# RWKV-7 and chunk-band attention trunk on one core: two pairs of heads side by side, and the key projections in one stretch

## The chip, the cores and the metric

One core of a Trainium2 chip runs the whole program. The metric is the device time of one execution in microseconds; of the kernel before there are three runs, 2769.82, 2777.21 and 2778.8 us, and one profiled execution.

## The reference

The input x is 256 tokens of 2048 elements in fp32. There are two layers. Layer 0 mixes over time (RWKV-7, 32 heads of 64) and has an MLP; then keys and values are projected once from the stream; layer 1 attends to those in a band of chunks and has another MLP. Each sub-layer stands behind an RMSNorm with shift and scale, and in front of a gate, all three from products c @ w_ada. The part that the change touches is this:

```python
    r = xr @ w_r
    k = xk @ w_k
    v = xv @ w_v
    w_log = -jax.nn.softplus(-(w0 + jnp.tanh(xw @ w1) @ w2)) - 0.5
    a = jax.nn.sigmoid(a0 + (xa @ a1) @ a2)
    g = jax.nn.sigmoid(xg @ g1) @ g2
    kk = heads(k * k_k)
    kk = kk / jnp.maximum(jnp.sqrt(jnp.sum(kk * kk, axis=-1, keepdims=True)), 1e-12)
    k = k * (1 + (a - 1) * k_a)
    decay = jnp.exp(-jnp.exp(heads(w_log)))
    ...
        sa = jnp.einsum('bhvk,bhk->bhv', S, -kk_t)
        S = (S * w_t[:, :, None, :] + sa[..., None] * (kk_t * a_t)[:, :, None, :]
             + v_t[..., None] * k_t[:, :, None, :])
        y = jnp.einsum('bhvk,bhk->bhv', S, r_t)
    ...
    y = y + jnp.sum(r_h * k_h * r_k.astype(jnp.float32), axis=-1, keepdims=True) * v_h
    y = y.reshape(B, T, D).astype(h.dtype) * g
    return y @ w_o
```

The step over time is computed in four chunks of 64 tokens per head: grams of the decayed keys, the inverse of a triangular 64x64 matrix per chunk and head (built from 32x32 blocks), and a state of 64x64 per head that is carried from chunk to chunk. The other sub-layers are not changed.

## The kernel before, in words

**Layout.** Features lie on the 128 partitions, tokens along the row: a matrix of 2048 features is 16 tiles (kt, KT = 16) of 128x256. A tile holds two heads, so there are 16 pairs of heads (`Pair`, NPAIR = 16).

**Dense projections.** Weights come from memory in pieces of 128x1024 fp32 (512 KB: eight kt, HK = 8, of one output tile), into a ring of six buffers named `raw`. ScalarE rounds a piece to `wH` (L360), VectorE makes the rest `wL` (L363), three buffers each. Activations are kept in such halves too (`aHL`, 16 KB a half on each partition, two buffers). For each kt TensorE takes one matmul of 512 columns with wH (L394) and one of 256 with wL (L395). In the output projection's first part the same is written as three matmuls of 256 columns (L383 to L385).

**The products c @ w_ada** (adaLN) go along everywhere as background work. A unit is one raw piece, loaded by the same queue (SP's) into the same ring, and one VectorE instruction (`acc`, L423). The program asks for units by `ada()` at fixed places and, where a result is needed, calls `ada_need`, which issues at that place all units still missing.

**Stages**, by the trace: the front with the v projection and the low-rank products up to 221.7 us; the loop over pairs and its drain up to 759; the rest of the output projection up to 835; MLP of layer 0 up to 1570; shared keys and values and attention up to 2060; MLP of layer 1 to the end.

**The loop over pairs.** Turn p runs four things side by side, each a generator that yields step by step: `late` of pair p-3 (16 steps: the four chunks in sequence, the norm, the gate), `invert` of pair p-2 (13 steps: grams, transposes, the inverse), `early` of pair p-1 (8 steps: decay, normalized key, the products, the bonus sum) and, as the dense part, the k and the r projection of pair p (16 steps of two kt). A turn has 16 slots. In each slot the generators advance by their share; `issue_after` ties the small matmuls of a slot behind the dense ones two slots before, and the dense ones behind the small ones, so that TensorE's queue alternates between a small group and two kt of dense work. From p = 2 on a turn asks for six adaLN units. Three further turns (p = 16 to 18) drain the pipeline and take steps of the output projection as dense work: the first halves of w_o for n = 0 to 7 and further kt of n = 0 to 3.

**Sums over a head** (in `early` for kk and the bonus, in `late` for the variance) multiply with a 128x128 matrix of ones in blocks (`bones`) in rounded halves: ScalarE writes the high part (L110), writes the same value again in fp32 (L113), POOL subtracts (L115, `sL`), and TensorE takes two matmuls of 256 columns (L120).

Of the kernel before, what the change touches and what calls it, by code (L numbers as in the profile page):

```python
# [11 lines left out]
F32 = mybir.dt.float32  # L12
F32R = mybir.dt.float32r
# [4 lines left out]
P = 128  # L18
D = 2048
# [13 lines left out]
        "w0", "a0", "k_k", "k_a", "r_k", "ln_w", "ln_b"]  # L33
# [3 lines left out]
def _constants():  # L37
# [23 lines left out]
    p = np.arange(P)  # L61
    bones = (p[:, None] // C == p[None, :] // C).astype(np.float32)
    put("bones", bones)
# [10 lines left out]
class Pair:  # L74
# [3 lines left out]
    EARLY = 8  # L78

    def __init__(self, body, j, v, tw, ta, tg, e01):  # L80
        self.b, self.j, self.v, self.tw, self.ta, self.tg, self.e01 = body, j, v, tw, ta, tg, e01
        self.heads = (slice(0, C), slice(C, P))

    def s(self, name="s", bufs=10):
        return self.b.pw.tile([P, T], F32, tag=name, bufs=bufs, name=name)

    def big(self, name, bufs):
        return self.b.pw.tile([P, 4, P], F32, tag=name, bufs=bufs, name=name)

    @staticmethod  # L90
    def ch(t):
        return t.rearrange("p (c t) -> p c t", t=C)

    def each(self, o, lhsT, rhs):
        for c in range(4):
            for K in self.heads:
                self.b.nc.tensor.matmul(o(c)[K], lhsT(c)[K], rhs(c)[K], start=True, stop=True)  # L97

    def tiles(self, o, lhsT, rhs, pairs):

        for c in range(4):
            for R, K in pairs:
                self.b.nc.tensor.matmul(o[QS[K], c, :], lhsT[QS[R], c, :], rhs[QS[R], c, :], start=True, stop=True,  # L103
                                        tile_position=(H * R, H * K))

    def parts(self, func, src, scale=1.0):

        nc, pw = self.b.nc, self.b.pw
# [6 lines left out]
        nc.gpsimd.tensor_tensor(out=L, in0=src, in1=H, op=ALU.subtract)  # L115
        return H, L

    def head_sums(self, ps, parts):
        for i, t in enumerate(parts):
            self.b.nc.tensor.matmul(ps, self.b.bones, t, start=(i == 0), stop=(i == 1))  # L120

    def early(self):
        b, nc, j, k, r, v, s, ch = self.b, self.b.nc, self.j, self.k, self.r, self.v, self.s, self.ch
        pw, vec, cst, e01 = b.pw, b.vec, b.cst, self.e01
        lw = pw.tile([96, 2, P], F32, tag="lw", bufs=2, name="lw")
        nc.sync.dma_start(out=lw, in_=b.d["lora2"][j, :96, 0:2])
        self.lg = pw.tile([P, 2, P], F32, tag="lg", bufs=2, name="lg")
        nc.sync.dma_start(out=self.lg, in_=b.d["lora2"][j, :, 2:4])
        z = b.psm()
        nc.tensor.matmul(z[:, 0:T], lw[:, 0, :], self.tw, start=True, stop=True)  # L130
        nc.tensor.matmul(z[:, T:2 * T], lw[:, 1, :], self.ta, start=True, stop=True)

        sw, a = s(), s()
        for o, at, b0 in ((sw, 0, "w0"), (a, T, "a0")):
            nc.vector.tensor_scalar(out=o, in0=z[:, at:at + T], scalar1=vec(b0, j), scalar2=-80.0,
                                    op0=ALU.add, op1=ALU.max)
            nc.scalar.activation(o, o, AF.Exp, scale=-1.0)
# [953 lines left out]
```

## Time and profile before

| | us |
|---|---|
| three runs | 2769.82, 2777.21, 2778.8 |
| median | 2777.21 |
| the profiled execution | 2773.6 |
| its span | 2771.8 |
| TensorE busy | 2653.9 (96%) |
| VectorE busy | 2087.3 (75%) |
| ScalarE busy | 1260.9 (45%) |
| POOL busy | 301.8 (11%) |
| moved by DMA | 662.60 MB, 239 GB/s on average |

A time in the text is the start within the span. A busy share is an average over stages; TensorE's ends are modelled, so the distance from one matmul's start to the next is the better measure of what one costs. "Granted clock" is the TensorE clock as a share of full speed in the stretch that is named. In the rows of the trace an idle time stands in brackets with what ended it; in a grouped row the number behind the bar is the group's busy time and the mean of one instruction in ns.

### The profile page before, as it was taken

What the parts mean: (1) busy time and instruction counts of PE and PEld (TensorE: products, weight loads), DVE (VectorE), ACT (ScalarE), POOL (GpSimd) and SP (SyncE); (2) the same over time, 40 slices, a digit from 0 to 9 for tenths busy, and PEclk for the clock granted to TensorE, in tenths of its full rate; (3) what the DMA queues carried; (4) which work ended last, traced back from release to release, by engine and by line L of the source; (5) the groups of instructions that cost most, each with busy time, mean ns of one, the idle gap of its engine ahead of it and who ended that gap; (6) DMA issues with size and microseconds to landing.
All of it is one profiled execution on the core that took longest, in us unless ns stands there. A gap on an engine that the chain in (4) does not pass through costs nothing.

```text
span 2771.8 us, 57644 instructions
## 1 busy us (share of the span) xinstructions
PE 2653.9 (96%) x23402; PEld 2217.6 (80%) x23402; DVE 2087.3 (75%) x3098; ACT 1260.9 (45%) x2214; POOL 301.8 (11%) x416
## 2 busy tenths in 40 slices
PE   6998999999998999999999899999989999999997
PEld 3677777777887888888888788877878888888886
DVE  4568778878889888888788896799786566665665
ACT  2345555556344434344344354465444344443444
POOL 0003443443220000000000200000100000000002
PEclk9999999999999999999999999999999999999999
DMA  9886556555687888888888868888876555555553
GB/s 297 269 281 193 169 171 196 176 176 162 216 302 243 298 308 305 300 314 296 299 306 302 304 218 282 268 293 268 279 242 216 187 186 186 187 183 189 185 188 122
DMA packets 217387, 662.60 MB, mean 239 GB/s; under 512 B 21408, under 2 KB 68896, under 8 KB 217120
## 3 DMA queue, kind: packets, MB, share of 16 engines
q1 hardware_dynamic: 215056, 656.36, 71.5%
q8 instruction: 184, 3.01, 0.4%
q10 hardware_dynamic: 2064, 2.54, 0.3%
q14 instruction: 83, 0.68, 0.1%
HBM read 656.72 MB, written 2.10 MB: 238 GB/s over the span
## 4 chain that ended last, share of the span: by engine, by line
PE 76%; DVE 9%; DMA 7%; issue 4%; POOL 1%; ACT 1%; DVEq 0%; SPq 0%; ACTq 0%; POOLq 0%
PE pj L394 40%; PE pj L395 20%; DMA raw<-w_ada 5%; DVE wL L363 3%; DVE acc L423 2%; PE iv L103 2%; PE gr L97 1%; DMA raw<-w_ada_kv 1%; PE m L625 1%; DVE un L504 1%; PE o L383 1%; PE ms L97 1%; POOL sL L115 1%; PE chn L276 1%; DVE aHL L506 1%
## 5 line engine op out<-in xcount | busy, mean ns | idle before, releaser
L394 PE MATMUL pj<-aHL,wH 128*128 128x512 f32 x3712 | 1353.5, 405 | 26.0 <-DVE aHL L506 22.4
L360 ACT CAST wH<-raw 128x1024 fp32r<-128x1024 f32 x772 | 807.0, 1047 | 949.4 <-PE pj L394 622.1
L363 DVE TENSOR_TENSOR wL<-raw,wH 128x1024 fp32r<-128x1024 f32 x772 | 946.1, 1228 | 290.7 <-ACT wH L360 288.8
L395 PE MATMUL pj<-aHL,wL 128*128 128x256 f32 x3712 | 1049.3, 283 | 7.5 <-DVE wL L363 7.2
L394 PEld LDWEIGHTS pj<-aHL,wH 128*128 128x128 f32 x3712 | 700.3, 189 | 199.2 <-issue 28.0
L394 PE MATMUL pj<-hHL,wH 128*128 128x512 f32 x2048 | 722.0, 397 | 4.5 <-DVE hHL L882 4.5
L395 PEld LDWEIGHTS pj<-aHL,wL 128*128 128x128 f32 x3712 | 705.3, 190 | 14.6 <-DVE wL L363 11.9
L395 PE MATMUL pj<-hHL,wL 128*128 128x256 f32 x2048 | 574.3, 281 | 4.6 <-DVE wL L363 4.5
L423 DVE SCALAR_TENSOR_TENSOR acc<-raw,ct,acc 128x1024 f32<-128x1024 f32 x360 | 470.4, 1307 | 139.8 <-DMA raw<-w_ada 104.0
L394 PEld LDWEIGHTS pj<-hHL,wH 128*128 128x128 f32 x2048 | 384.3, 188 | 97.9 <-DVE hHL L882 6.7
L395 PEld LDWEIGHTS pj<-hHL,wL 128*128 128x128 f32 x2048 | 386.8, 189 | 8.1 <-DVE wL L363 7.7
L482 POOL TENSOR_TENSOR ss<-ss,sq 128x256 f32<-128x256 f32 x56 | 65.0, 1160 | 1599.7 <-ACT sq L481 1599.4
L901 DVE SCALAR_TENSOR_TENSOR x<-pj,mod,x 128x256 f32<-128x256 f32 x256 | 123.1, 481 | 51.7 <-PE pj L395 48.8
L881 ACT CAST hHL<-t 128x256 fp32r<-128x256 f32 x128 | 51.4, 403 | 67.6 <-DVE t L880 67.3
L625 PE MATMUL m<-rawa,crep 128*32 128x256 f32 x512 | 47.4, 449 | 17.5 <-DMA rawa<-w_ada 16.9
L481 ACT ACTIVATE sq<-x 128x256 f32<-128x256 f32 x60 | 25.0, 418 | 70.5 <-DVE x L901 39.6
L880 DVE SCALAR_TENSOR_TENSOR t<-t 128x256 f32<-128x256 f32 x128 | 53.9, 422 | 3.0
L882 DVE TENSOR_TENSOR hHL<-t,hHL 128x256 fp32r<-128x256 f32 x128 | 53.4, 418 | 0.6 <-ACT hHL L881 0.5
L862 DVE TENSOR_TENSOR t<-pj,t 128x256 f32<-128x256 f32 x128 | 53.2, 417 | 0.0
L239 POOL TENSOR_TENSOR al<-da,csts 128x128 f32<-128x128 f32 x64 | 40.7, 647 | 67.4 <-PE iv L103 62.7
L861 ACT COPY t<-pj 128x256 f32<-128x256 f32 x128 | 46.6, 366 | 0.0
L685 PE MATMUL t<-aHL,wH 128*128 128x256 f32 x128 | 38.1, 298 | 5.8 <-DVE v L693 3.6
(230 smaller groups left out, 2483.0 us busy)
## 6 DMA issues: line engine op xcount, KB each, us to landing
raw<-w_ada SPq DMA_DIRECT2D x320, 512.0 KB, 4.7
raw<-w_up SPq DMA_DIRECT2D x256, 512.0 KB, 4.9
raw<-w_down SPq DMA_DIRECT2D x256, 512.0 KB, 4.3
rawa<-w_ada SPq DMA_DIRECT2D x64, 512.0 KB, 6.8
raw<-w_ada_kv SPq DMA_DIRECT2D x64, 512.0 KB, 5.4
raw<-w_k SPq DMA_DIRECT2D x32, 512.0 KB, 4.2
raw<-w_r SPq DMA_DIRECT2D x32, 512.0 KB, 4.7
raw<-w_o SPq DMA_DIRECT2D x32, 512.0 KB, 5.2
```

Of the source, the lines that this page charges most:

```text
L97: self.b.nc.tensor.matmul(o(c)[K], lhsT(c)[K], rhs(c)[K], start=True, stop=True)
L103: self.b.nc.tensor.matmul(o[QS[K], c, :], lhsT[QS[R], c, :], rhs[QS[R], c, :], start=True, stop=True, tile_position=(H * R, H * K))
L360: nc.scalar.copy(Hf, raw)
L363: eng.tensor_tensor(out=Lf, in0=raw, in1=Hf, op=ALU.subtract)
L394: nc.tensor.matmul(ps, H[:, i, :], a(kt), start=(kt == 0), stop=False)
L395: ins = nc.tensor.matmul(ps[:, 0, :], L[:, i, :], a(kt)[:, 0, :], start=False, stop=(kt == KT - 1))
L423: nc.vector.scalar_tensor_tensor(out=acc, in0=raw, scalar=ck, in1=acc, op0=ALU.mult, op1=ALU.add)
L482: (eng or nc.gpsimd).tensor_tensor(out=self.ss, in0=self.ss, in1=sq, op=ALU.add)
L625: nc.tensor.matmul(ps[g:g + 32, part, :W], crep[:, kt, :], raw[:, i, :], start=(part == 1 and kt < 4), stop=(part == 0 and kt >= KT - 4), ...
L880: nc.vector.scalar_tensor_tensor(out=t, in0=t, scalar=0.0, in1=t, op0=ALU.max, op1=ALU.mult)
L882: nc.vector.tensor_tensor(out=h[:, 1, :], in0=t, in1=h[:, 0, :], op=ALU.subtract)
L901: nc.vector.scalar_tensor_tensor(out=x, in0=ps[:, i, :], scalar=self.mods[(layer, 5)][:, n:n + 1], in1=x, op0=ALU.mult, op1=ALU.add)
```

## The change

`Pair` becomes `Quad`: two pairs side by side in tiles of 512 columns, eight quads. `early` and `invert` are one generator, `prep` (20 steps); `late` keeps 16 steps, with each chunk's step for both pairs. A turn has 20 slots; turns p = 0 to 9 run late of quad p-2, prep of quad p-1 and the r projections of quad p, two pairs' worth.

All 16 k projections run ahead of the turns without small work between, and their result stays in a new tile of 16 KB a partition; every 11th of their kt asks for an adaLN unit (23 in all), and every turn from p = 0 on for six. When they are done, the room of their operand (a buffer of `aHL`) becomes `hold`, in which two quads in flight keep kr, mk, bk and ar. To make room elsewhere the ring `raw` has four buffers in place of six up to the output projection; from there on `more_raw` adds a second pool, of four buffers in the output projection and the MLPs and of two in attention.

Sums over a head are two fp32 matmuls of 64x64 ones with 512 columns, without halves. The biases w0 and a0 are a 97th row of the low-rank weights. The gram of 128 columns is taken in two halves, `ms` has three PSUM buffers in place of two, and some small matmuls are pinned to program order. The drain is two turns long: w_o's first halves for n = 0 to 3, then further kt of those and the first halves of n = 4 and 5; n = 6 and 7 are left whole to the output projection. `ada_need` for the MLP's shift and scale stands behind the output projection.

The core of the diff:

```diff
@@ class Pair -> class Quad
+    PREP, LATE = 20, 16
+    def pairs(self, *ts):
+
+        for i in range(2):
+            yield (2 * self.q + i,) + tuple(t[:, i * T:(i + 1) * T] for t in ts)
...
-        H, L = (pw.tile([P, T], F32R, tag=n, bufs=2, name=n) for n in ("sH", "sL"))
-        nc.scalar.activation(H, src, func, scale=scale)
-        if func != AF.Copy:
-            t = self.s("pt", 2)
-            nc.scalar.activation(t, src, func, scale=scale)
-            src = t
-        nc.gpsimd.tensor_tensor(out=L, in0=src, in1=H, op=ALU.subtract)
-        return H, L
-
-    def head_sums(self, ps, parts):
-        for i, t in enumerate(parts):
-            self.b.nc.tensor.matmul(ps, self.b.bones, t, start=(i == 0), stop=(i == 1))
+    def head_sums(self, t):
+        ps = self.b.psm()
+        for K in self.heads:
+            self.b.mm(ps[K], self.b.cst("ones")[K, 0:C], t[K], start=True, stop=True)
+        return ps
...
+        e = pw.tile([P, 4 * T], F32, tag="e", bufs=1, name="e")
+        sw, a = e[:, 0:2 * T], e[:, 2 * T:4 * T]
+        for o, t, n in ((sw, self.tw, 0), (a, self.ta, 1)):
+            z = b.psm()
+            for i in range(2):
+                b.mm(z[:, i * T:(i + 1) * T], lw[:, n, i, :], t, start=True, stop=True)
+            nc.vector.tensor_scalar(out=o, in0=z, scalar1=-80.0, scalar2=None, op0=ALU.max)
+        nc.scalar.activation(e, e, AF.Exp, scale=-1.0)
+        yield
...
+        nc.gpsimd.tensor_tensor(out=bh, in0=a, in1=e2, op=ALU.mult)
+        for j, o in self.pairs(a):
+            nc.gpsimd.tensor_scalar(out=o, in0=o, scalar1=-1.0, scalar2=vec("k_a", j), op0=ALU.add, op1=ALU.mult)
...
@@ class Body
-    RAW_BUFS = 6
     W_BUFS = 3
-    DRAIN_STEPS = (14, 14, 16)
-    ADA_SLOTS = (1, 3, 6, 9, 11, 14)
+    SLOTS = 20
+    ADA_SLOTS = (1, 4, 8, 11, 14, 18)
+    def raw_tile(self):
+
+        self.nraw += 1
+        if self.more and self.nraw % (self.more[1] + 4) >= 4:
+            return self.more[0].tile([P, HK * P], F32, tag="raw", bufs=self.more[1], name="raw")
+        return self.wp.tile([P, HK * P], F32, tag="raw", bufs=4, name="raw")
...
-            self.ada_need((0, 2), (0, 4), (0, 3))
-            self.out_proj(self.pp, "w_o", self.y_hl, (0, 2), self.o_ps)
+            self.ada_need((0, 2))
+            with self.more_raw(4):
+                self.out_proj(self.pp, "w_o", self.y_hl, (0, 2), self.o_ps)
+            self.ada_need((0, 4), (0, 3))
...
-            weights = iter([d[n][j] for j in range(NPAIR) for n in ("w_k", "w_r")])
+            weights = iter([d[n][j] for n in ("w_k", "w_r") for j in range(NPAIR)])
...
+            for n, _ in enumerate(proj_steps(range(KT), xk, lambda i: k[:, i, :])):
+                if n % 11 == 10:
+                    self.ada()
+            hold = self.hp.tile([P, 2, KT * T], F32, tag="aHL", bufs=2, name="hold")
+            NQ_ = NPAIR // 2
+            quads = [Quad(self, q, k, v, tw, ta, tg, hold[:, q % 2, :]) for q in range(NQ_)]
...
-            for p in range(NPAIR + 3):
+            for p in range(NQ_ + 2):
                 live = []
+                if p >= 2:
+                    live.append([quads[p - 2].late(), Quad.LATE, 0])
+                if 1 <= p <= NQ_:
+                    live.append([quads[p - 1].prep(), Quad.PREP, 0])
+                if p < NQ_:
+                    dense = [r_steps(quads[p]), 2 * KT, 0]
...
+                else:
+                    dense = [out_steps([(n, HK, KT - 2) for n in range(4)] + [(n, 0, HK) for n in (4, 5)]), 20, 0]
...
-                    if slot in self.ADA_SLOTS and p >= 2:
+                    if slot in self.ADA_SLOTS:
                         self.ada()
```

How the instructions move shows at three places. First TensorE in a full turn, from its first matmuls on the low-rank product (`ms<-tw,lw`). In the names, `pj` is the dense sum, `chn`, `py` and `zs` belong to the chunks in `late`, `ms` is a PSUM tile shared by the small products, `iv` the inverse. Before:

```order
L130 MATMUL ms<-tw,lw 128x256
L131 MATMUL ms<-ta,lw 128x256
L394 MATMUL pj<-aHL,wH 128x512
L395 MATMUL pj<-aHL,wL 128x256
L394 MATMUL pj<-aHL,wH 128x512
L395 MATMUL pj<-aHL,wL 128x256
L283 MATMUL chn<-g,uf_2204 64x64 x2
L286 MATMUL py<-mk,bk 64x64 x2
L97 MATMUL ms<-csts,s 64x64 x16
L394 MATMUL pj<-aHL,wH 128x512
L395 MATMUL pj<-aHL,wL 128x256
```

and now, the last rows ahead of the gram (`ms<-hold,bh`), with the bonus sum (`ms<-s,csts`) in front of it (L358 is the helper `mm`, through which all small matmuls go):

```order
L358 MATMUL chn<-zs,hold 64x64 x2
L358 MATMUL py<-hold,zs 64x64 x2
L358 MATMUL chn<-g,uf_2207 64x64 x4
L358 MATMUL chn<-hold 64x64 x4
L358 MATMUL chn<-sa,hold 64x64 x4
L358 MATMUL py<-hold,sa 64x64 x4
L358 MATMUL py<-hold 64x64 x4
L358 MATMUL py<-hold,zs 64x64 x2
L358 MATMUL ms<-s,csts 64x512 x2
L358 MATMUL ms<-hold,bh 64x64 x32
```

Groups of small matmuls are twice as large and stand behind each other, with fewer dense pieces between them. From the first dense matmul of the loop to the first one of the output projection, TensorE's queue changes between dense, 64x64 and 32x32 work 580 times before and 317 times now, and in the drain 108 and 73 times.

Second, VectorE in a turn now, from the sum of squares of the key (`s<-ms`), which it reads behind the decay's scan, to the first half of the bonus product (`s<-r,vecs,e`). `e<-e,k` is the key times its factor, `hold<-r,e` the decayed r, `acc` an adaLN unit, `zs` the state of `late`:

```order
L151 TENSOR_SCALAR s<-ms 128x512
L176 TENSOR_TENSOR hold<-r,e_2204 128x8x64
L166 SCALAR_TENSOR_TENSOR e<-e,k 128x512
L305 SCALAR_TENSOR_TENSOR zs<-zs,pc,chn 128x64
L180 TENSOR_TENSOR kh<-e,s 128x512
L305 SCALAR_TENSOR_TENSOR zs<-zs,pc,chn 128x64
L453 SCALAR_TENSOR_TENSOR acc<-raw,ct,acc 128x1024
L161 SCALAR_TENSOR_TENSOR s<-s 128x512
L162 SCALAR_TENSOR_TENSOR s<-s 128x512
L305 SCALAR_TENSOR_TENSOR zs<-zs,pc,chn 128x64
L165 SCALAR_TENSOR_TENSOR s<-k,vecs,s 128x256 x2
L179 SCALAR_TENSOR_TENSOR s<-r,vecs,e 128x256
```

The bonus product stands behind the key's factor (L166, it waits for POOL), the normalized key (L161 to L165) and, of other work, an adaLN unit and the state of `late`, all in one queue; a unit (L453) and a weight's rest (L393) stand shortly ahead of these rows too. Before, the same steps were instructions of 256 columns, twice as many.

Third, SP's queue of loads where MLP 0 passes from its first half (w_up) to its second (w_down). Before:

```order
L350 DMA raw<-w_up 128x1024 x2
L350 DMA raw<-w_ada_kv 128x1024 x2
L350 DMA raw<-w_up 128x1024 x2
L350 DMA raw<-w_ada_kv 128x1024
L350 DMA raw<-w_down 128x1024 x2
```

and now:

```order
L380 DMA raw<-w_up 128x1024 x2
L380 DMA raw<-w_ada 128x1024 x2
L380 DMA raw<-w_up 128x1024 x2
L380 DMA raw<-w_ada 128x1024 x8
L380 DMA raw<-w_ada_kv 128x1024
L380 DMA raw<-w_ada 128x1024
L380 DMA raw<-w_down 128x1024 x2
```

Eight units of the gate that MLP 0 needs are still missing there and go in front of the first piece of w_down. Before attention's output projection eleven units stand in front in the same way; before, none did at either place.

More of the change, by code (lines that the diff above doesn't have):

```diff
@@ L205, in invert, with gram @@
+        def half(name, bufs):
+            return pw.tile([P, 8, H], F32, tag=name, bufs=bufs, name=name)
+        def gram(src, n):
+            ps = ch(b.psm())
+            self.each(ps, lambda c: ch(src)[:, c, :], lambda c: kr[:, c, C * n:C * n + C])
+            return ps
+        ui = every("ui", P)
         ts = []
```

352 lines of the change are left out of this document (175 added, 177 removed).

## The prediction

> **What bounds the kernel now.** First the page: its span, the busy times and the shares of the chain that ended last.
>
> ```profile
> span 2771.8 us, 57644 instructions
> PE 2653.9 (96%) x23402; PEld 2217.6 (80%) x23402; DVE 2087.3 (75%) x3098; ACT 1260.9 (45%) x2214; POOL 301.8 (11%) x416
> ...
> PE 76%; DVE 9%; DMA 7%; issue 4%; POOL 1%; ACT 1%; DVEq 0%; SPq 0%; ACTq 0%; POOLq 0%
> ```
>
> The chain is three quarters TensorE, so TensorE's own cost is asked first. The table by stages follows (us; busy time and instructions of PE, PEld, DVE, ACT and POOL; granted clock, DMA share, GB/s): the loop's start, its full turns, the drain, the rest of the output projection, the middle of MLP 0.
>
> ```profile
> 221.70:310.40 88.70, 80.98 (x1170) 64.54 (x1170) 74.71 (x133) 49.85 (x127) 35.06 (x43) 0.98 0.62 199
> 310.40:653.20 342.80, 336.21 (x6396) 260.59 (x6394) 273.08 (x511) 182.84 (x508) 143.80 (x187) 0.99 0.56 177
> 653.20:759.00 105.80, 105.00 (x2013) 87.18 (x2012) 87.26 (x154) 51.59 (x146) 29.92 (x44) 1.00 0.58 187
> 759.00:835.00 76.00, 66.69 (x445) 57.95 (x444) 61.69 (x70) 31.32 (x42) 17.44 (x14) 0.93 0.89 301
> 1035.00:1535.00 500.00, 493.57 (x3221) 428.19 (x3220) 421.69 (x519) 215.20 (x277) 7.70 (x6) 1.00 0.88 304
> ```
>
> The full turns are TensorE's (336.2 of 342.8 us busy), with a DMA share of 0.56: room for loads. The output projection has both TensorE and DMA near full, and MLP 0 has TensorE full at a DMA share of 0.88 and 304 GB/s, where an extra load costs time if it comes at once. Loop and drain take 759.0 − 221.7 = 537.3 us. What a turn is made of shows in TensorE's timeline (start, duration, line, tiles, count):
>
> ```profile
> 407.12 0.50 PE L394 MATMUL pj<-aHL,wH 128*128 128x512 f32 x1
> 407.46 0.28 PE L395 MATMUL pj<-aHL,wL 128*128 128x256 f32 x1
> 407.57 0.40 PE L394 MATMUL pj<-aHL,wH 128*128 128x512 f32 x1
> 407.81 0.28 PE L395 MATMUL pj<-aHL,wL 128*128 128x256 f32 x1
> 408.02 0.33 PE L293 MATMUL chn<-bk 64*64 64x64 f32 x4
> 408.18 0.28 PE L295 MATMUL chn<-sa,bk 64*64 64x64 f32 x4
> 408.30 0.28 PE L304 MATMUL py<-ar,sa 64*64 64x64 f32 x4
> 408.51 0.45 PE L103 MATMUL iv<-tt,al 32*32 32x32 f32 x32
> 408.90 0.50 PE L394 MATMUL pj<-aHL,wH 128*128 128x512 f32 x1
> ```
>
> From 407.12 to 408.02 two kt of dense work take 0.90 us; then a small group of 64x64 matmuls starts its parts 0.16, 0.12 and 0.21 us apart, and one of 32x32 takes 0.39. Unbroken dense work in MLP 1:
>
> ```profile
> L394 PE MATMUL pj<-hHL,wH x150: 395/398/403, 2159.9 to 2212.6; 128*128 128x512 f32 x150
> ```
>
> 149 distances in 52.7 us: 0.354 us per kt, so 0.71 for two. Between small groups two kt thus cost 0.19 more, and the small group's last part 0.09 to 0.12 more than its middle: about 0.31 us a round trip. This, and no engine's rate, is what the loop has to give. By such distances TensorE's instructions of loop and drain come to 503 us: 512 kt 181, 344 round trips 107, the small matmuls 143 (four of 64x64 by 0.12, 32 of 32x32 by 0.39), w_o's matmuls 31, 64 low-rank products of 0.43 (quoted below) 27, head sums 11, adaLN's sums 3. Of 537, 34 are left for waits and slow clock. The waits view of that stretch names the largest (total, times, longest), two rows of the timeline show one each (in brackets the idle time), and the windows the clock around them:
>
> ```profile
> PE py L120 <- POOL sL L115: 7.7, 4, 2.2
> ```
>
> ```profile
> 367.23 0.39 PE L120 MATMUL py<-sL,bones 128*128 128x256 f32 x1 [2.09 <-POOL sL L115]
> 429.83 0.38 PE L120 MATMUL py<-sL,bones 128*128 128x256 f32 x1 [1.47 <-POOL sL L115]
> ```
>
> ```profile
> 365.00:367.60 2.60, 0.51 (x4) 0.38 (x3) 1.81 (x2) 0.12 (x1) 2.54 (x4) 1.00 0.87 255
> 367.60:371.00 3.40, 3.40 (x25) 2.91 (x23) 1.21 (x3) 1.39 (x4) 1.45 (x4) 0.51 0.75 251
> 429.80:433.40 3.60, 3.57 (x58) 2.92 (x59) 2.19 (x4) 2.06 (x6) 1.80 (x5) 1.00 0.75 271
> 616.30:619.90 3.60, 3.54 (x24) 3.17 (x25) 1.21 (x3) 1.39 (x4) 1.83 (x6) 0.57 0.73 228
> ```
>
> TensorE waits 7.7 us for POOL's part of a head sum. After 2.09 us of idling the clock is 0.51 for 3.4 us, behind the longest wait, 2.2 (up to 616.3), it is 0.57, after 1.47 it stays at 1.00. A drop costs half of 3.4 = 1.7 us.
>
> **The change part by part.**
>
> *Alternations.* The order of TensorE's queue has 580 changes between dense, 64x64 and 32x32 work before and 317 after, in the drain 108 and 73: 298 fewer, 149 round trips by 0.31: **−46 us**. This is on the bounding engine.
>
> *Head sums.* Before, 48 of them by two matmuls of 256 columns as cheap as L395 (0.12 from start to next): 11.5 us. The new fp32 sum of 512 columns isn't in the trace; the nearest row is the fp32 product at the head of `early`:
>
> ```profile
> L130 PE MATMUL ms<-tw,lw x24: 379/431/483, 310.4 to 653.5; 96*128 96x256 f32 x24
> ```
>
> 0.43 us for 256 columns, so 0.86 for 512 if the two heads run side by side as other 64x64 pairs do: 24 × 0.86 = 20.6, **+9** (twice that if they don't run side by side: +30; 11.5 if fp32 were as cheap as the halves: 0). I take the row it is nearest to. In return POOL's subtraction goes, and with it the 7.7 us and two drops of 1.7: **−11**.
>
> *Moved work.* The first halves of w_o for n = 6 and 7 leave the drain: 16 kt by three matmuls of 0.12, **−6**. They come back in the output projection with TensorE at 66.7 of 76 us and DMA at 0.89: **+5** (3 if DMA alone counts, for two pieces, to 6). The other small matmuls have the same columns as before, two pairs at a time: 0.
>
> *The remaining 23 us* over the sum are 4.6% of 503; they go with mixed work, of which 133 us fall away or become unbroken: **−6**.
>
> *The k stretch.* 256 kt by 0.354 = 91 us. VectorE has 32 `wL` and 23 adaLN units there:
>
> ```profile
> L363 DVE TENSOR_TENSOR wL<-raw,wH 128x1024 fp32r<-128x1024 f32 x768 | 944.2, 1232 | 288.9 <-ACT wH L360 287.1
> L423 DVE SCALAR_TENSOR_TENSOR acc<-raw,ct,acc 128x1024 f32<-128x1024 f32 x360 | 470.4, 1307 | 139.8 <-DMA raw<-w_ada 104.0 <-DMA raw<-w_ada_kv 34.7
> ```
>
> 39 + 30 = 69 us, so it fits under 91. SP's queue must bring 55 pieces: 28.8 MB at MLP 0's 304 GB/s are 95 us. A piece takes this long from issue to landing (median):
>
> ```profile
> raw<-w_ada SPq DMA_DIRECT2D x320, 512.0 KB, 4.7
> ```
>
> With 2.3 us of ACT and DVE behind it a buffer is bound 7 us, and a ring of four gives a piece each 1.75 us, 96 us. What stands ready at the start shortens it, a later release lengthens it to 99: I take 95, **+4**. (By the same 7 us the ring of six gives one each 1.2.)
>
> *The chain in a turn.* From the first low-rank product to the bonus sum that stands ahead of the grams there is one dependent chain. Before, 16 slots of two kt lay beside a chain of 256 columns. Now, by the distances above, TensorE has 15.3 us of instructions between the two (16.3 with the loop's 7% over its sum). The rows that price the chain, busy and mean ns of one:
>
> ```profile
> L148 DVE TENSOR_TENSOR_SCAN s<-csts,s 128x256 f32<-128x256 f32 x16 | 11.3, 708 | 1.6 <-ACT s L142 1.5
> L261 DVE TENSOR_TENSOR mk<-gr,csts 128x512 f32<-128x512 f32 x16 | 11.0, 686 | 1.9 <-PE gr L97 1.0
> L861 ACT COPY t<-pj 128x256 f32<-128x256 f32 x128 | 46.6, 366 | 0.0
> L229 ACT COPY bk<-ms 128x512 f32<-128x512 f32 x16 | 9.3, 581 | 2.6 <-PE ms L97 2.5
> L150 ACT ACTIVATE e<-s 128x256 f32<-128x256 f32 x16 | 6.7, 417 | 9.5 <-DVE s L148 9.3
> L142 ACT ACTIVATE s<-s,csts 128x256 f32<-128x256 f32 x16 | 8.1, 505 | 0.0
> L164 POOL TENSOR_TENSOR bh<-s 128x256 f32<-128x256 f32 x16 | 15.7, 983 | 1.5 <-ACT s L152 1.5
> L162 POOL TENSOR_SCALAR s<-s,vecs 128x256 f32<-128x256 f32 x16 | 14.9, 931 | 0.0
> L169 DVE SCALAR_TENSOR_TENSOR s<-k,vecs,s 128x256 f32<-128x256 f32 x16 | 7.6, 478 | 0.0
> ```
>
> DVE at 512 columns costs 0.69, ACT 0.58 (0.37 for 256, so 0.21 for each further 256, and 1.05 and 1.14 for 1024 by the exponential's 0.42 and the logarithm's 0.51). Product 1.7; maximum 0.69; exponential 1.05; logarithm 1.14; exponential 0.72; two scans 1.42; two exponentials 1.25. From there POOL's product (2 × 0.98) and key factor (2 × 0.93) take 3.8 us, and beside it three ACT and four DVE steps of the norm 4.1. Then factor, kr, bh, kr 2.75 and the bonus 0.96: 15.8 us, with a dozen handoffs, which no quoted row prices and for which I put 0.13 each, 17.4. VectorE works through one queue in which an adaLN unit (1.31), `wL` (1.23) and `zs` stand among these steps: 21.7 if they all fall on the chain. TensorE then stands 1.1 to 5.4 us a turn, with the grams and all dense pieces of the rest of the turn queued behind the bonus sum; in the middle 3.2. Eight turns: **+26** (9 to 43). By the drops quoted a stall of this size can halve the clock, as it did after 2.09 and 2.2 us but not after 1.47; I put a drop behind every second: 4 × 1.7 = **+7** (0 to 14).
>
> The Trainium skill, "TensorE: Matmul & The Clock Gate", section "HAM oscillation — how this bites in real kernels", asks for TensorE idle gaps below about 3.4 us. By that rule the middle stall would cost no clock, and the forecast would be 7 us lower; the trace differs, its drop follows 2.09 us.
>
> *adaLN units.* Counted in the order: before, 102 units ride in the loop and 118 are done at the end of the output projection; now 23 + 60 = 83 and 99. 128 are needed before MLP 0's first w_down, and by then 120 are there: eight are forced, and eleven ahead of attention's output projection. By TensorE's buffers (a piece is 2.8 us of work, three of wH and wL wait) they show only with what VectorE puts ahead of the next `wL`, about four steps of 1.2 to 1.3: 5 us each, **+10** (0, if the ring covers, to 19 × 1.72 = 33, if none hides). More raw buffers after that: −3 to 0, **−2**.
>
> The sum: −46 + 9 − 11 − 6 − 6 + 4 + 26 + 7 = −23 for loop and drain, 514 us. Then +5 + 10 − 2 = +13; in all −10. The profiled execution has 2773.6 us (2771.8 of span), the median is 2777.2; from the median the forecast is **2767 us**, from the profiled one 2764.
>
> **The rivals.**
>
> *The chain is hidden.* If adaLN steps and `wL` fall beside the waits for ACT and POOL, and the bonus isn't late, the 26 and 7 go: 2734. For it: 17.4 is only 1.1 over TensorE's work, and late's matmuls stand in between. Against it: VectorE's queue is in order, and 75% busy.
>
> *The chain sets every turn* (slower). POOL's products cost more while VectorE works, as one line's two forms show:
>
> ```profile
> L208 POOL TENSOR_TENSOR s<-kh,pc 128x256 f32<-128x256 f32 x16 | 20.6, 1284 | 2.5 <-DVE kh L178 2.5
> L208 POOL TENSOR_TENSOR s<-bh,pc 128x256 f32<-128x256 f32 x16 | 12.2, 760 | 84.9 <-DVE bh L174 84.9
> ```
>
> 1284 against 760 ns. At that price the chain's product takes 2.6 in place of 2.0, and one more adaLN unit falls on it: 21.7 + 0.6 + 1.3 less 16.3 is a stall of 7.3, with a drop 9.0, eight times 72 in place of 33: 2806. It decides against the change from 5.4 us a turn on ((33 + 10) / 8). For it: nothing of the next quad can run ahead in TensorE's queue. Against it: POOL has fewer instructions than before.
>
> The Trainium skill, "GPSIMD Engine Reference", section "1. Specifications", says that POOL shares its SBUF interfaces with VectorE and meets its two-input instructions there. By that rule the slower row is the one to expect in this chain; the trace agrees with its 1284, though not for every product.
>
> *The loads set the pace.* The k stretch takes 99 (+4), and no forced unit hides (+23): 2794. For it: DMA at 0.88 to 0.89 in MLP 0 and the output projection. Against it: most forced loads overlap TensorE's backlog.
>
> **How the numbers follow.** Forecast 0.36, hidden chain 0.27, chain in every turn 0.25, loads 0.12. The likeliest's own range is 2749 to 2787. With all cases, 8 in 10 lie between 2728 and 2806. A difference under 0.3%, 8 us, can't be told. The forecast's cases give 0.18 faster, 0.14 same, 0.04 slower; the hidden chain 0.27 faster; the chain in every turn 0.01, 0.04 and 0.20; the loads 0, 0.03 and 0.09: faster 0.46, same 0.21, slower 0.33.
>
> **What would show it.** In the profile after: the k stretch ending 91 to 99 us after 221.7; TensorE's idle rows inside full turns, ahead of the bonus sum (L179 as releaser), with 3 us and a clock drop behind some; full turns of 48 to 51 us; a TensorE wait for `wL` of 5 us at the first w_down, and at attn_w_o. A turn near 45 shows the hidden chain, one over 52 the slower case. The forecast is wrong at its root if alternations cost less than 0.31 in the wider groups, or if the new sums cost 30 us.

## The result

| | us | runs |
|---|---|---|
| before | 2774.3 median (2769.82 to 2778.8) | 4 |
| after | 2903.97 median (2895.24 to 2909.32) | 4 |

The ratio is 1.0464, with a 95% interval of 1.0429 to 1.0499: the change costs 130 us, where 10 were to be gained. The profiled execution of after took 2900.47 us. Its page begins:

```profile
span 2898.6 us, 57618 instructions
PE 2668.4 (92%) x23882; PEld 2230.3 (77%) x23882; DVE 2066.1 (71%) x2893; ACT 1204.7 (42%) x1869; POOL 188.9 (7%) x264
```

TensorE's busy time is 15 us longer than before (2668.4 against 2653.9), the span 127: it waits. By the starts of the dense matmuls, the stages are:

| stage, from its first dense matmul to the next one's | before | after | difference | predicted |
|---|---|---|---|---|
| front | 221.7 | 218.6 | −3.1 | 0 |
| loop, drain (to the output projection's undivided part) | 559.0 | 637.8 | +78.8 | −23 |
| rest of the output projection | 60.8 | 68.5 | +7.7 | +5 |
| MLP 0 | 753.5 | 770.2 | +16.7 | +8 with the next two |
| shared keys and values, attention | 431.1 | 465.2 | +34.1 | in the +8 |
| MLP 1 | 745.7 | 738.3 | −7.4 | in the +8 |

The prediction ended the loop with the last small matmuls (759.0 before). By that cut loop and drain end at about 828 and cost some 72 us more, and what follows costs some 14 more up to MLP 0.

The windows of after (as in the prediction: busy time of PE, PEld, DVE, ACT, POOL, clock, DMA share, GB/s) are the k stretch, the way to the next low-rank product, two full turns, the drain, the output projection:

```profile
218.60:323.90 105.30, 96.79 (x577) 82.36 (x578) 71.31 (x84) 41.30 (x61) 0.99 (x2) 0.95 0.78 258
323.90:346.10 22.20, 19.25 (x91) 14.30 (x91) 15.55 (x16) 5.10 (x7) 0.00 (x0) 0.92 0.82 277
456.90:518.40 61.50, 49.22 (x1119) 38.58 (x1117) 31.57 (x53) 21.50 (x43) 9.98 (x15) 0.89 0.26 78
518.40:577.70 59.30, 49.22 (x1183) 38.08 (x1181) 37.30 (x58) 21.60 (x43) 13.81 (x15) 0.94 0.38 117
759.30:856.00 96.70, 85.98 (x1623) 73.81 (x1622) 62.17 (x100) 37.58 (x77) 15.54 (x18) 0.93 0.45 144
856.00:930.00 74.00, 64.32 (x413) 54.95 (x412) 63.14 (x81) 31.55 (x44) 13.45 (x11) 0.93 0.83 291
```

A full turn takes 59 to 62 us where 48 to 51 were forecast. In the two shown the granted clock is 0.89 and 0.94 and the DMA share 0.26 and 0.38: neither TensorE nor the memory is full. What TensorE waits for in five such turns, from the waits view (total, times, longest):

```profile
PE chn L358 <- ACT sa L285: 20.9, 7, 6.6
PE ms L358 <- DVE s L179: 12.1, 5, 2.5
PE iv L358 <- issue: 10.1, 6, 2.5
PE py L358 <- DVE zs L305: 9.9, 3, 8.1
```

With small ones the waits are 58 us, 11.6 a turn; TensorE waits for no `wH` and no `wL` there. The prediction had the second row alone (12.1 in five turns, 2.4 each, against 3.2 forecast), and the largest is another: `sa`, a copy of ScalarE in `late`. Over the whole loop and drain, though, the predicted wait is the largest, and half of it is one stall in the first turn with `prep` (the waits view for 218 to 857, and the stall in the timeline):

```profile
PE ms L358 <- DVE s L179: 33.8, 7, 17.4
367.07 1.97 PE L358 MATMUL ms<-s,csts 64*64 64x512 f32 x4 [17.40 <-DVE s L179]
```

The timelines of three engines show why TensorE stands 6.62 us in front of 472.76. TensorE, ScalarE, VectorE:

```profile
465.23 0.91 PE L358 MATMUL ms<-csts,v 64*64 64x64 f32 x22
472.76 0.69 PE L358 MATMUL chn<-hold 64*64 64x64 f32 x8 [6.62 <-ACT sa L285]
```

```profile
463.48 1.04 ACT L390 CAST wH<-raw 128x1024 fp32r<-128x1024 f32 x1 [0.86 <-PE pj L424]
471.39 0.63 ACT L144 ACTIVATE e<-s 128x512 f32<-128x512 f32 x1 [6.87 <-DVE s L142]
471.93 0.61 ACT L146 ACTIVATE s<-s 128x512 f32<-128x512 f32 x1
472.45 0.26 ACT L285 ACTIVATE sa<-chn 128x128 f32<-128x128 f32 x1
```

```profile
460.17 0.29 DVE L302 COPY zs<-chn 128x128 f32<-128x128 f32 x1 [1.84 <-PE chn L358]
468.89 1.28 DVE L453 SCALAR_TENSOR_TENSOR acc<-raw,ct,acc 128x1024 f32<-128x1024 f32 x1 [8.42 <-DMA raw<-w_ada]
470.09 1.27 DVE L142 TENSOR_TENSOR_SCAN s<-csts,e 128x256 f32<-128x256 f32 x2
```

Read from below. VectorE stands 8.42 us at an adaLN unit (L453) until its load lands. The scan of `prep` (L142) is behind the unit in VectorE's queue. ScalarE's exponential (L144) needs the scan and stands 6.87 us. `sa` (L285) is behind the exponential in ScalarE's queue, though all it reads has long been ready, and TensorE needs `sa`. Background work that nothing here depends on holds three engines, through their queues alone. Over 346 to 759 us VectorE waits this much for units' loads, and before (221 to 759) this much:

```profile
DVE acc L453 <- DMA raw<-w_ada: 46.2, 16, 8.4
```

```profile
DVE acc L423 <- DMA raw<-w_ada: 0.8, 1, 0.8
```

Of after's 46.2 us, 32.1 are four waits, of 8.42, 8.18, 8.17 and 7.35 us. Each of the four units was issued as the first load behind a turn's `lw`, the low-rank weights, and took 11.0 to 12.2 us to land, where the median of `raw<-w_ada` on the page is 5.2. For the unit issued at 457.63, 0.36 us behind its `lw`, the first row has its landing (least, median and most of this one load), the second what the DMA did meanwhile:

```profile
DMA to landing us min/median/max: 11.2/11.2/11.2
462.00:468.00 6.00, 4.14 (x68) 3.23 (x62) 0.00 (x0) 1.35 (x3) 0.00 (x0) 1.00 0.07 26
```

A DMA share of 0.07 is one engine of 16, and it moves 26 GB/s. In the trace's packets `lw` is 97 rows of 2 KB that go one after another from 458.17 to 467.28. Of the unit's 128 packets of 4 KB 120 have started by 461.1, and the last eight come behind the last row of `lw`. In the kernel before `lw` has 96 rows of 1 KB and landed in 1.9 to 3.7 us from 340 on. The 97th row, the biases, is new; no run loads the new `lw` in another way, so that the number of rows is the reason is likely but not shown.

The other 14 us are waits of at most 2.5 us, most of them at units issued behind a piece of w_r. Where SP's queue stands shows in its timeline, and in what it waits for, after and before:

```profile
440.85 0.33 SPq L380 DMA_DIRECT2D raw<-w_ada  x1
444.45 2.78 SPq L380 DMA_DIRECT2D raw<-w_r  x2
457.63 15.20 SPq L380 DMA_DIRECT2D raw<-w_ada  x3
```

```profile
SPq L380 <- DVE wL L393: 93.3, 18, 15.8
```

```profile
SPq L350 <- DVE wL L363: 80.1, 36, 6.9
```

From 457.63 three units' loads are spread over 15.2 us. In a turn r needs four weights' pieces, four in 60 us where k and r together took four in 31. A piece lies in its raw buffer until VectorE makes its `wL`, for which a buffer must be given back by TensorE; so the release that SP waits for is up to 15.8 us off where it was up to 6.9, and units stand behind it. At 457.63 that was not the reason: the buffer was free, and SP had stood at `lg` and `lw` for TensorE to be done with them.

### The profile page after: what moved, and what is told of

Its sections match the earlier page's. It is cut to its first block, busy times and chain, and to the rows that moved or that the text cites. A ratio compares the mean times of both kernels' runs of the same rounds, so it can differ in the third digit from the quotient of the medians.

```text
span 2898.6 us, 57618 instructions
## 1 busy us (share of the span) xinstructions
PE 2668.4 (92%) x23882; PEld 2230.3 (77%) x23882; DVE 2066.1 (71%) x2893; ACT 1204.7 (42%) x1869; POOL 188.9 (7%) x264
## 3 DMA queue, kind: packets, MB, share of 16 engines
q1 hardware_dynamic: 212896, 656.38, 68.5%
## 5 line engine op out<-in xcount | busy, mean ns | idle before, releaser
L393 DVE TENSOR_TENSOR wL<-raw,wH 128x1024 fp32r<-128x1024 f32 x772 | 940.9, 1221 | 359.5 <-ACT wH L390 357.5
L425 PE MATMUL pj<-aHL,wL 128*128 128x256 f32 x3744 | 1062.4, 284 | 11.2 <-DVE wL L393 10.9
L424 PEld LDWEIGHTS pj<-aHL,wH 128*128 128x128 f32 x3744 | 711.4, 190 | 219.7 <-issue 29.0
L425 PEld LDWEIGHTS pj<-aHL,wL 128*128 128x128 f32 x3744 | 716.3, 191 | 21.4 <-DVE wL L393 19.8
L453 DVE SCALAR_TENSOR_TENSOR acc<-raw,ct,acc 128x1024 f32<-128x1024 f32 x360 | 470.2, 1306 | 177.1 <-DMA raw<-w_ada 158.9
L358 PE MATMUL ms<-s,csts 64*64 64x512 f32 x64 | 27.9, 777 | 33.8 <-DVE s L179 33.8
L923 DVE SCALAR_TENSOR_TENSOR t<-t 128x256 f32<-128x256 f32 x128 | 53.9, 422 | 2.5
L358 PE MATMUL chn<-hold 64*64 64x64 f32 x448 | 31.3, 241 | 21.7 <-ACT sa L285 21.2
```

The costliest lines, as they stand in the source:

```text
L358: ins = self.nc.tensor.matmul(*args, **kw)
L393: eng.tensor_tensor(out=Lf, in0=raw, in1=Hf, op=ALU.subtract)
L424: nc.tensor.matmul(ps, H[:, i, :], a(kt), start=(kt == 0), stop=False)
L425: ins = nc.tensor.matmul(ps[:, 0, :], L[:, i, :], a(kt)[:, 0, :], start=False, stop=(kt == KT - 1))
L453: nc.vector.scalar_tensor_tensor(out=acc, in0=raw, scalar=ck, in1=acc, op0=ALU.mult, op1=ALU.add)
L923: nc.vector.scalar_tensor_tensor(out=t, in0=t, scalar=0.0, in1=t, op0=ALU.max, op1=ALU.mult)
```

## The experiments

The cause is taken apart first: is it the units (e1), their loads or their VectorE time (e5), the size of the ring (e2, e4), its order (e3, e7) or SP's queue (e6, e8)? "Turn" below is the mean of the five last turns, from the third start of L129 to the eighth; after has 60.4.

**e1, no units in the turns.**

```diff
-    ADA_SLOTS = (1, 4, 8, 11, 14, 18)
+    ADA_SLOTS = ()
```

> The adaLN units of the turns are left out of the turns; all that are missing are done in one block behind the loop, so the whole time grows and only the loop's turns are read. In the changed kernel the five turns from 456.9 to 759.3 us take 60.5 us each. Theory R (ring): a unit waits in VectorE's queue for a load that came late because the ring of four buffers was full, and the scan, the state and the rest wait behind it. Without units the turns take 47 to 50 us. Theory C (chains): the steps of prep and late hold each other up in the in-order queues by their own lengths. The turns stay at 57 us or more.

Whole time 2918.89 us (the missing units come in one block behind the loop, 144 us there); turn 51.6, loop and drain 569.3 in place of 637.8. Five turns:

```profile
430.70:688.80 258.10, 233.64 (x5578) 180.09 (x5577) 130.16 (x242) 108.12 (x218) 53.30 (x75) 0.94 0.16 53
```

The clock is 0.94, and TensorE's waits for `sa` are 1.9 us in place of 20.9. Units cost 9 us a turn.

**e2, six raw buffers in the stretch and the turns.** The tile of keys is half as large, and `more_raw(2)` is opened around the loop; half of the quads read other quads' keys.

> The tile of the keys is half as large (later quads read the wrong keys), and its room gives two more raw buffers in the k stretch and the turns: six as before. R: the k stretch falls from 105 to 91 to 95 us and the turns from 60.5 to at most 52; the loads of the units no longer end VectorE's idle time (46 us from 346 to 759 in the changed kernel). C: the turns stay at 57 or more.

Turn 57.6, k stretch 103.3, loop and drain 617.1. VectorE still waits 28.6 us for units' loads in 380 to 740. Size helps by less than a third.

**e3, two of the four for weights, two for units.**

```diff
+        n = "rawu" if (unit if self.apart else i % 4 >= 2) else "raw"
+        return self.wp.tile([P, HK * P], F32, tag=n, bufs=2, name="raw")
```

> The same four raw buffers, but in the turns two of them are for weights and two for adaLN units, so that a unit doesn't wait behind a weight's piece that waits for TensorE. R in this form (the order in the ring, not its size): turns of at most 52 us, k stretch unchanged at 105, whole time 2850 to 2870. If the size is what counts: turns of 57 or more, whole time above 2890. C: 57 or more as well.

2893.54 us median (1.042 of before, 1.0327 to 1.0514); turn 55.6, loop and drain 625.9. Half of what was expected.

**e4, the kernel before with four.**

```diff
-    RAW_BUFS = 6
+    RAW_BUFS = 4
```

> The kernel before with four raw buffers in place of six, everywhere. R: loop and drain (558.9 us from the first k matmul to the first dense one of the output projection) grow by 30 us or more, with VectorE waiting for units' loads. C: by 10 or less; the old loop isn't sensitive to the ring.

2885.84 us, but loop and drain stay (556.1 against 559.0); MLP 0 pays, 848.8 in place of 753.5. The ring's size alone doesn't hurt the old loop, in which a weight's buffer comes free each few microseconds. So theory R in its plain form falls: it takes the ring and the turn with little dense work.

**e5, units without loads.** In the turns `acc` reads a part of the keys that is there already; the modulation is computed from wrong weights for these units.

```diff
-                raw = self.raw(w[kt * P:(kt + 1) * P, half * n_:(half + 1) * n_])
+                raw = self.resident
```

> The units in the turns keep their VectorE instruction, but read a tile that is there already; their loads are left out (the modulation is wrong for it, and later stages load the rest). Theory L (late loads): a unit costs turn time because VectorE's queue stands at it until its load lands. Turns fall from 60.5 to 50 to 53 us, near the 51.1 without units. Theory V (VectorE time): six instructions of 1.3 us in the in-order queue, in front of the steps of prep and late, cost the time themselves. Turns stay at 57 to 61.

2843.73 us; turn 51.6, loop and drain 577.3. Five turns, and TensorE's waits in them:

```profile
444.60:702.40 257.80, 232.44 (x5706) 178.60 (x5705) 170.50 (x275) 108.36 (x218) 57.37 (x75) 0.96 0.16 53
```

```profile
PE iv L358 <- issue: 5.8, 5, 2.1
PE ms L358 <- DVE s L179: 6.8, 3, 2.5
PE chn L358 <- ACT sa L285: 1.1, 3, 0.4
```

VectorE is as busy per unit as in after, and the turn is that of e1. In these turns it is the loads that cost 9 us, not VectorE's 1.3 us each; in loop and drain they cost 60. The wait for the bonus product (L179) stays, 1.4 a turn, and the one for `sa` is nearly gone. In the first turn with `prep` VectorE's time counts too: the stall at the bonus sum is 17.4 us in after, 13.8 in e5 and 8.4 in e1, and loop and drain take 8 us more in e5 than in e1.

**e6, e7, e8: where the loads stand.** e6 is e3 with the units' loads issued by POOL (`nc.gpsimd.dma_start`). e7 has half a tile of keys like e2 and gives four buffers to weights, two to units. e8 is after with `lw` in two buffers and `lg` loaded at the end of `prep`.

> Of four raw buffers two are for units in the turns, and the units' loads are issued by POOL's queue, past SP's. L, by SP's order (a weight's load that waits for its buffer holds the units behind it): turns of at most 54 us. If POOL's own steps of prep now wait behind a load, or V holds: 57 or more.

> Half a tile of keys (later quads read the wrong keys) makes room for six raw buffers; in the turns four are for weights, so that SP's queue seldom stands at a weight, and two for units. L: turns of at most 54 us where six shared buffers gave 58. V: 57 or more.

> The low-rank weights lw have two buffers in place of one, and lg is loaded at the end of prep: SP's queue no longer waits at these two for TensorE (43 us between 346 and 759). L with this cause: turns fall by 3 to 5 us, to 55 to 57, and VectorE waits for units' loads less than 46 us. Otherwise 59 to 61.

e6: turn 53.9, loop and drain 624.2 (2894.35 us). e7: 54.7 and 613.1 (2877.91). e8: 60.0 and 644.8 (2919.6). Two buffers apart and POOL's queue together regain 6.5 of the 9 us (the buffers alone, in e3, 4.8), more buffers for weights 5.7, an earlier place for the low-rank loads nothing. e8 has three waits of 7.7 to 7.9 us left, each at a unit issued 0.35 us behind `lw` that took 10.5 to 10.7 us to land: SP stands less at `lw`, but its rows move as before. Its k stretch got longer (116.0 us); why stays open. VectorE's waits for units in 380 to 740 fall, but don't vanish; in e6:

```profile
DVE acc L457 <- DMA raw<-w_ada: 17.2, 16, 4.0
```

The second turn of e6 and e7 got longer in return (69.5 and 66.0 in place of 63.1). Which share of the lateness is the transfer of `lw`, which SP's order and which the two buffers a unit must wait for isn't separated by a run.

**e9, the k stretch.** After with the first two quads' low-rank loads queued behind the stretch's weights, and no units in turn 0.

```diff
+        with b.tc.issue_after(b.k_end) if self.q < 2 else nullcontext():
-                    if slot in self.ADA_SLOTS:
+                    if slot in self.ADA_SLOTS and p >= 1:
```

> The first loads of low-rank weights are tied behind the k stretch's loads in SP's queue, and turn 0, which has dense work alone, asks for no units. Theory Q: the 105 us of the k stretch (91 to 95 by TensorE or DMA) come from SP's queue standing at these loads, whose room is still read, with the weights of k behind them; and the 22 us from the first r matmul to the first low-rank product (11.4 of matmuls) from six units in a turn too short for their loads. k stretch 95 to 99, then 13 to 16 us. Rival: the ring of four throttles the whole stretch, 103 to 106. Six units more are missing later.

2897.67 us. The two slow projections at the head (8.6 and 9.4 us in after) are 5.6 and 5.7, but others are slow now: the stretch is 101.8 where 95 to 99 were expected, and from the first r matmul to the low-rank product's maximum (L129) it is 24 us: TensorE stands 5.2 us for the low-rank weights that were tied. The stand at the head is explained; the rest of the stretch's 10 us over the forecast is not, but after's and e9's traces have one slow projection more, of 11.0 and 12.4 us, in which TensorE stands 3.0 and 4.3 us for a unit's `acc`. The turn is 57.9 here, loop and drain 618.4; MLP 0 (779.4) and what follows took most of that back.

**e10, all mendings.** e6 with e9's ties and nine units a turn, so that none is forced later.

> All mendings together: units by POOL's queue with two raw buffers of their own in the turns, nine a turn from turn 1 on, so that none is forced at w_down or attn_w_o, and the low-rank loads tied. If late loads, forced units and the stand at the low-rank loads are the causes, loop and drain take 600 to 620 us in place of 638, MLP 0 and attention come back to within 8 us each of the kernel before, and the whole time is 2815 to 2850. If nine units a turn bring the stall back, turns stay at 58 or more and the time above 2860.

2918.9 us median (1.0492, 1.0456 to 1.0527): worse than after. Turn 57.3, loop and drain 654.3. POOL's queue now waits for the units' buffers, and steps of `prep` stand behind that; TensorE's stall at the bonus product in the first turn with `prep`, 17.4 us in after, is 24:

```profile
POOL raw L385 <- DVE acc L458: 87.1, 37, 5.7
```

```profile
PE ms L359 <- DVE s L180: 37.6, 5, 24.0
```

MLP 0 and attention didn't return to the old times either (782.9 and 459.1 us in the profiled execution, the longest of four with 2940.62 us), though no unit is forced; why isn't settled. Moving loads past one in-order queue put them into another.

**e11, forced units in the kernel before.**

```diff
-    ADA_SLOTS = (1, 3, 6, 9, 11, 14)
+    ADA_SLOTS = (1, 4, 7, 10, 13)
-            self.ada_need((0, 2), (0, 4), (0, 3))
+            self.ada_need((0, 2))
             self.out_proj(self.pp, "w_o", self.y_hl, (0, 2), self.o_ps)
+            self.ada_need((0, 4), (0, 3))
```

> The kernel before with five units a turn in place of six and the changed place of ada_need, so that by the order seven or eight units are forced ahead of the first w_down and twelve ahead of attn_w_o, as in the changed kernel. Theory F: it is the forced and shifted units that cost MLP 0 and attention their 49 us (16.6 and 31.9): here +12 to +20 and +22 to +35. Rival: the two pools of raw buffers cost it, which this kernel does not have: +10 at most, the sum predicted.

2803.08 us. MLP 0 grows by 23.1 us (753.5 to 776.6), attention with its shared keys by 19.3 (431.1 to 450.4), while the loop gains 9.2. The windows of MLP 0's first half and of the q projection with the scores, of before, of after and of e11:

```profile
841.50:1212.40 370.90, 365.58 (x2369) 317.30 (x2370) 315.13 (x401) 159.46 (x204) 0.00 (x0) 0.99 0.86 293
1785.80:1918.30 132.50, 131.49 (x907) 103.33 (x896) 126.77 (x269) 78.71 (x207) 7.54 (x56) 1.00 0.86 289
```

```profile
924.90:1307.20 382.30, 373.95 (x2433) 322.29 (x2434) 328.70 (x412) 158.90 (x204) 0.00 (x0) 0.98 0.87 300
1894.40:2050.20 155.80, 144.82 (x996) 110.89 (x994) 142.46 (x298) 84.19 (x225) 7.22 (x56) 0.95 0.84 273
```

```profile
829.50:1212.60 383.10, 371.60 (x2433) 321.29 (x2434) 325.08 (x410) 159.31 (x205) 0.00 (x0) 0.98 0.86 294
1795.20:1952.30 157.10, 144.12 (x996) 109.76 (x994) 142.49 (x298) 84.34 (x225) 7.70 (x56) 0.96 0.82 271
```

The old kernel with the units moved has the new kernel's times there (383 and 157 against 382 and 156). By the sums it explains 42 of the 51 us that MLP 0 and attention lost, 23.1 where MLP 0 lost 16.7 and 19.3 of attention's 34.1. These are single executions: e13, which leaves MLP 0 as it was, has 762.5 us there in place of 753.5, so a stage's time is good to about 9 us. What the shared keys and values lost (190.8 to 199.3) doesn't come back in e11 (189.1) and stays open.

**e12, e13, e14: single parts in the kernel before.** e12 opens `more_raw(2)` around the two MLPs, e13 takes the new `head_sums` on 256 columns, e14 both.

> The kernel before with two more raw buffers, eight, in the two MLPs alone (the room is free there). In the changed kernel MLP 1 took 738.3 us with eight in place of 745.7 with six; in the kernel before with four it took 747.2, and MLP 0 gained 94 us from four to six. Prediction's term: -2 (0 to -3). Theory: MLP 1 falls by 4 to 8, MLP 0 by 0 to 8, the whole by 4 to 16.

> One part alone: the kernel before with the new head sums, two fp32 matmuls of 64x64 ones on 256 columns per pair, without halves, second pass and POOL's subtraction. The prediction priced this at +9 for TensorE and -11 for the waits that go: -2 for loop and drain (559.0 before). If TensorE's two matmuls don't run side by side: +20. If the waits alone count: -11.

> The kernel before with eight raw buffers in the MLPs and the new head sums. The sum of the two: 6 to 18 us under the kernel before if the sums gain, 4 to 12 if they are neutral, no gain if the fp32 sums cost 10.

e12: 1.0002 (0.9989 to 1.0015): nothing. e13: 2783.41 us in one run, loop and drain 564.7 against 559.0 (and 562.2 in e12, whose loop is unchanged). e14: 1.0033 (1.002 to 1.0046), 9 us slower. So the sums cost, where −2 was forecast. In e13 POOL's stop is gone from TensorE's waits, of which the largest two are now 2.2 and 2.1 us, but a sum of 64x64 ones is one more change from dense work, where the old one was dense itself: 612 changes in place of 580, 16 round trips, by the 0.31 us of the prediction some 5 us that the term of +9 didn't hold. No version that ran beats the kernel before.

## Why the prediction was wrong

**What held.** The sum over TensorE's instructions: a dense pair of kt, a small group and a head sum in a turn of after start like this:

```profile
458.48 0.50 PE L424 MATMUL pj<-aHL,wH 128*128 128x512 f32 x1
458.81 0.28 PE L425 MATMUL pj<-aHL,wL 128*128 128x256 f32 x1
458.93 0.40 PE L424 MATMUL pj<-aHL,wH 128*128 128x512 f32 x1
459.17 0.28 PE L425 MATMUL pj<-aHL,wL 128*128 128x256 f32 x1
459.37 0.45 PE L358 MATMUL chn<-hold 64*64 64x64 f32 x8
459.66 0.40 PE L358 MATMUL chn<-sa,hold 64*64 64x64 f32 x8
459.89 0.40 PE L358 MATMUL py<-hold,sa 64*64 64x64 f32 x8
460.12 1.03 PE L358 MATMUL ms<-s,csts 64*64 64x512 f32 x4
461.08 0.50 PE L424 MATMUL pj<-aHL,wH 128*128 128x512 f32 x1
```

Two kt take 0.89 us (0.90 before), the groups of eight start 0.29, 0.23 and 0.23 apart, and the sum takes 0.96 with its change of mode (0.86 without, as priced). Of a turn's 60.4 us 11.6 are waits, and the slow clock (0.90 on average, 6.1) cost 4.5 outside of them: 44.3 are left for TensorE's own instructions. Before, eleven turns took 342.8 us (310.4 to 653.2) with 10.0 of waits and slow clock, so two took 60.5 without these, and 49.2 without the 11.3 of k's 32 kt. So TensorE gains 4.9 us a turn, where the prediction's alternations outside the drain (−41), less its 9 for the sums, make 4 over eight turns: the gain was real, and was given back. The price of the chain held too. In the first turn with `prep`, where no `late` runs beside it, the way from the first maximum of the low-rank product (346.1) to the bonus sum (367.1) is 21.0 us with the units, and 15.8 in e1 without them; less the product's 1.7, the prediction's 21.7 and 17.4 are 20.0 and 15.7. The drop of the clock after stalls also held; only there were more stalls. The windows behind three of them, of 6.62, 2.45 and 2.55 us (the clock is the third number from the end):

```profile
472.80:476.20 3.40, 3.40 (x38) 3.09 (x39) 2.57 (x5) 2.38 (x4) 2.34 (x3) 0.50 0.64 190
604.10:607.50 3.40, 3.40 (x38) 2.16 (x40) 0.83 (x2) 0.00 (x0) 1.84 (x2) 0.53 0.03 12
553.90:557.30 3.40, 3.40 (x111) 2.71 (x110) 2.03 (x3) 0.65 (x2) 0.60 (x1) 1.00 0.07 11
```

Of the twelve stalls over 2.1 us in the five turns eleven were followed by a clock of 0.50 to 0.67 over 3.4 us. The rule of the Trainium skill ("TensorE: Matmul & The Clock Gate", section "HAM oscillation — how this bites in real kernels") is to have no TensorE gaps above about 3.4 us; here 2.45 us was enough, so the measurement decides.

**What failed: the stall in a turn, +26 and +7.** The step "in the middle 3.2. Eight turns" priced a queue of durations: `acc` at 1.31 us a piece, as if its load were always there. The profile before had VectorE wait for units in the loop 0.8 us, and the prediction took that over into a turn in which the ring is smaller and each weight's piece lies in it twice as long. It had even worked out the ring (7 us a buffer, four buffers), but for the k stretch alone. And it gave the biases as a 97th row no price: the four longest of VectorE's waits, 32.1 of 46.2 us, are at units whose last rows came behind `lw`. Measured: 11.6 of waits and 4.5 of slow clock outside of them a turn, 16 in place of 4. e5 gives the part of the units' loads, 60 us of loop and drain; without them a turn is 51.6, next to the forecast's 48 to 51. How much of the 60 us is `lw`'s 97 rows no run shows. That VectorE's stop reaches TensorE through ScalarE's queue (`sa`) was not among the steps at all. Nor were the turns alike: the bonus product's wait, put at 3.2 in each of eight turns (26 in all), was 17.4 in the first, where TensorE had no `late` to cover it, 4.3 in the second, and 2.4 a turn in the five last. That its total of 33.8 came near the 26 is luck. Of the rivals, the chain in every turn came nearest in size (72 us of stall and clock), by another cause.

**The k stretch and the first turns.** 95 us were forecast for the stretch (91 and +4), 105.3 measured, and the way from the first r matmul to the next low-rank product took 22 us in place of 11.4. The low-rank loads at its head are a part (e9); TensorE's waits in the stretch are 3.0 us for a unit's `acc`, 2.9 for a `wH` and 2.6 for `wL`. In e5 the turn behind that has 60.7 us where every turn was put at the same price; its TensorE instructions are 5 us more than in a later one.

**The forced units, +10.** By its own bounds 0 to 33, the lower third was taken, since TensorE's buffers would cover most. e11 shows some 42 us for the same move in the old kernel, with the scatter named there. The likely reason, not shown by itself, is that the loads of 19 units, 1.72 us each, aren't hidden in stages with a DMA share of 0.86 (the rows of before above), and that stops come on top. If the 42 hold, the upper end of the range was low as well.

**Smaller terms.** Output projection +5, measured +7.7, and some +14 by the prediction's own cut; in the trace after, 7.2 us of that are two waits for its `wH`. More raw buffers −2: MLP 1 took 7.4 us less in after's profile, but e12 shows no gain by buffers, and between single executions a stage scatters as much. Head sums and the waits they removed, −2 forecast: +5.7 in one run of the loop (e13), +9 for the whole with a tight interval (e14).

## What to carry to other kernels

Before a background load is moved into another schedule, ask for its consumer: what stands behind it in that engine's in-order queue, and is the load surely there by then? Look at how long the late load took to land, and at the DMA share meanwhile, before you blame its queue: a share of one engine in 16 points at a transfer ahead of it that isn't spread, here that of a tile of 97 rows. A ring shared by weights and background loads is only as fast as its slowest release, and with half the dense work per unit of time a weight's piece blocks it longer (up to 15.8 us here, 6.9 before). Work that is pushed out of a stage with room (DMA share 0.6) into stages that are balanced at 0.88 is safer priced at its full transfer time than at what buffers might cover.

## What was not expected of the hardware

A load of 97 rows went through one DMA engine: 97 packets of 2 KB one after another, 9.1 us, while the 512 KB behind it had all but a sixteenth of its packets under way within 3.5 us. The loads of 96 rows (before) and of 128 rows are spread over the engines in the traces. No run here varies the rows alone.

TensorE stops for a while within long runs of small matmuls, though nothing that the profile shows ended the stop ("issue"). In a run of 64 matmuls of 32x32, which goes at some 10 ns each, of after:

```profile
497.36 0.64 PE L358 MATMUL iv<-u,xs 32*32 32x32 f32 x51
500.32 0.32 PE L358 MATMUL iv<-u,xs 32*32 32x32 f32 x13 [2.32 <-issue]
```

The run breaks off after 51 matmuls for 2.32 us. In after such stops in runs of 32x32 add up to 15.5 us in 12 times, in the loop and drain before to 0.9 in two, with runs half as long; they stay in e1 and e5. Their cause was not tested.
